# The scan's two gate projections as seven block products per pair of chunks

## The chip, the cores and the metric

The kernel runs on one core of one Trainium2 chip, as one launch. The metric is device microseconds of that launch, the median of several runs. Five engines of the core work beside each other: PE (TensorE, matmuls; PEld is its weight load), DVE (VectorE), ACT (ScalarE), POOL (GpSimd) and SP (SyncE, which here only issues DMAs). Data lives in DRAM, in SBUF (128 partitions) and in PSUM, where matmuls write; the kernel divides it in eight banks of 128 x 512 float32.

## The reference, cut to what matters

One layer over 4096 positions of width 1024. The input is normed and projected; half of the columns (group A) go through a matrix memory with four heads of 128, scanned in chunks of 128 positions in both directions; the other half (group B) through windowed attention. What the change touches are the columns `o_a` and `z_a` of the projection, 512 each:

```python
hn = rms_norm(x, norm_w)                      # [1, 4096, 1024]
proj = hn @ w_in                              # columns 1536:2048 are o_a, 2048:2560 z_a, 2560:3072 z_b (after a reorder of w_in's columns)
h = sigmoid(o_a) * (h_fwd + h_bwd)            # h_fwd, h_bwd: mLSTM over chunks of 128
h = h * rsqrt(mean(h * h) + EPS) * mhn_w      # per head
y_a = h * silu(z_a)
y_b = windowed_gqa(q_b, k_b, v_b) * silu(z_b)
x + concat([y_a, y_b]) @ w_out                # and a last rms_norm
```

So for a pair of chunks the gates are a product of a 2 x 2 block matrix with another: rows are the two chunks, the inner blocks the halves of the 1024 inputs, and columns o and z.

## The kernel before, in words

The kernel's matmuls of 128x512 take fp32r operands, and to keep float32's accuracy each operand is split into a high part (a cast by ACT) and a low part (what the cast left, by DVE or POOL), and each product is three matmuls: one with the low input, one with the low weight, one with both high parts. A full product of 128 positions with 512 columns is 8 blocks of K times 3, 24 matmuls of 128x512 that add up in one PSUM bank.

The program has four stages. Pass 1 (to about 590 us) norms the input in groups of 256 positions, splits it (`splits`, tiles `xT`), stores both parts in DRAM (`xT_d`), and does the projections of group B and its attention. Pass 2 (about 590 to 1167) goes backward over eight blocks of 512 positions: v, q and k of group A, the short convolution, and the state of the backward scan. Pass 3, the scan, is 32 chunks forward. The tail (from about 1700) does the gates of group B (`zunits`) and the output projection, which already works with seven block products per pair (`OutPair`).

In the scan a chunk n has these steps. `scores` multiplies lq and lk into a bank (S), and DVE multiplies S into the decays E in both directions. `heads` makes, per head, num = W x state + E x v for both directions (4 matmuls of 128x129); DVE takes the denominators (r), ACT scales the forward half into hs, DVE adds the backward one, multiplies the gate o in and, after the norm (ss3, with a power on POOL), the gate z. `yout` transposes hs on PE (yp), ACT copies it (ya), POOL stores it. `state` carries the running state CC on, `weigh_q` makes W = W x lq for two chunks ahead, and `proj` makes the gates: 24 matmuls op and 24 zp per chunk (L1262), a tanh on ACT and, for z, one DVE operation (L1272).

PE's order is the order in which the code issues (a manual schedule); `interleave` deals the steps of a chunk (`pieces`) evenly between its matmuls (`fill`). The other engines' orders are set by a list scheduler. All loads of the scan go through SP's queue in program order, and a load whose buffer isn't free holds up all behind it. Buffers are pools of tiles by tag: `x4` (`xtile`, 4 KB per partition) and `w8` (`wtile`, 8 KB) are shared by all passes; lq, lk, lv and lkf have two buffers each.

The inputs of the gates (`xs`, both parts) come from DRAM per pair of chunks, those of the first pair are still in SBUF; the weights (`w3`) are split by ACT and DVE at the end of pass 2 (`next_weights`). The weights of z_b, which the tail needs, are split a little at a time over the chunks (`zweight`, `zsplit`).

```python
c.psum({"pj": 2, "n": 2, "c": 1, "y": 1})      # PSUM: gates, num (2 banks each), S, yp
```

## Time and profile before

| what | value |
|---|---|
| median of 3 runs | 2185.28 us (2182.06 to 2185.89) |
| the profiled execution, its span | 2182.1 us |
| PE busy | 2156.9 us (99%), 12226 matmuls |
| DVE / ACT / POOL busy | 1416.9 (65%) / 1079.3 (49%) / 567.7 (26%) |
| op and zp in the scan (L1262), busy | 202.3 and 187.9 us, 720 records each |
| xs loads (SP) | 120 of 256 KB, 6.6 us from issue to landing |

The profiled execution took as long as its span, the least of the three times. Matmuls overlap, so the busy time of one (0.39 to 0.41 us for 128x512) is longer than the distance to the next; some records are missing (720 of 768). The chain that ended last is the one to read first, then the busy times by stage. A number in the column of idle time tells what an engine waited for, and costs nothing where the engine has time.

### The profile page before, as it was taken

The numbers are of one execution on the slowest core, as the hardware profiler recorded it, in microseconds if no ns is written. First come the engines' busy times: TensorE is split into PE (matmuls) and PEld (weight loads), VectorE is DVE, ScalarE is ACT, GpSimd is POOL, SyncE is SP. The second block draws the span as 40 slices with busy tenths as digits, with TensorE's granted clock in tenths as the row PEclk, the third lists the DMA queues.
The fourth block names the chain that finished last, engine by engine and source line by source line (L and its number), as shares of the span: only waits on it lengthen the run. The fifth ranks groups of instructions, "written<-read, shape, count | busy, mean of one in ns | idle before, by whom it ended". The sixth has DMA issues, their size and how long they took to land. (4 is left out here: it accounts for less than half of the span.)

```text
span 2182.1 us, 34919 instructions
## 1 busy us (share of the span) xinstructions
PE 2156.9 (99%) x12226; PEld 1872.4 (86%) x12226; DVE 1416.9 (65%) x3041; ACT 1079.3 (49%) x2650; POOL 567.7 (26%) x918
## 2 busy tenths in 40 slices
...
GB/s 277 158 171 147 128 173 122 130 124 64 102 148 78 141 163 135 62 160 160 113 163 230 290 259 238 211 253 225 214 238 188 329 359 283 181 177 191 193 191 147
DMA packets 249132, 398.96 MB, mean 183 GB/s; under 512 B 21979, under 2 KB 128475, under 8 KB 248956
## 3 DMA queue, kind: packets, MB, share of 16 engines
...
## 5 line engine op out<-in xcount | busy, mean ns | idle before, releaser
L932 PE MATMUL up<-xb,w 128*128 128x512 f32 x1344 | 338.4, 396 | 0.0
L1443 PE MATMUL o<-wo,yo 128*128 128x512 f32 (+1 forms) x1356 | 312.8, 393 | 0.0
L1443 PEld LDWEIGHTS o<-wo,yo 128*128 128x128 f32 x1356 | 253.2, 188 | 59.7
L932 PEld LDWEIGHTS up<-xb,w 128*128 128x128 f32 x1344 | 243.8, 188 | 47.2
L950 DVE SCALAR_TENSOR_TENSOR qk<-U,cw,qk 128x512 f32<-128x512 f32 x256 | 189.2, 752 | 91.1 <-ACT qk L948 85.8
L548 PE MATMUL qp<-xT,wqb 128*128 128x256 f32 x1536 | 242.4, 288 | 0.1
L548 PEld LDWEIGHTS qp<-xT,wqb 128*128 128x128 f32 x1536 | 214.2, 190 | 8.7 <-DVE wqb L319 0.5
L1262 PE MATMUL op<-w,xs 128*128 128x512 f32 x720 | 202.3, 408 | 0.0
L1262 PE MATMUL zp<-w,xs 128*128 128x512 f32 x720 | 187.9, 401 | 0.7 <-DVE z L1272 0.7
L905 PE MATMUL v2p<-w,xb 128*128 128x512 f32 x672 | 157.6, 395 | 0.0
L1262 PEld LDWEIGHTS zp<-w,xs 128*128 128x128 f32 x720 | 130.9, 189 | 27.4 <-DVE z L1272 1.1
L414 DVE TENSOR_TENSOR pt<-tp,pt 128x512 fp32r<-128x512 f32 x188 | 129.1, 687 | 37.7 <-ACT pt L413 35.2
L905 PEld LDWEIGHTS v2p<-w,xb 128*128 128x128 f32 x672 | 126.1, 188 | 30.1 <-DMA xb<-xT_d 0.5
L391 ACT ACTIVATE s<-s,NG 128x320 f32<-128x320 f32 (+1 forms) x256 | 139.8, 548 | 11.4 <-DVE NG L389 10.8
L1262 PEld LDWEIGHTS op<-w,xs 128*128 128x128 f32 x720 | 126.7, 189 | 21.4
L413 ACT CAST pt<-tp 128x512 fp32r<-128x512 f32 x188 | 110.5, 588 | 69.9 <-PE tp L411 67.6
L382 DVE CUSTOM_DVE_ANT_0 s<-sp,G 128x320 f32<-128x320 f32 (+1 forms) x256 | 122.2, 478 | 32.6 <-PE sp L379 29.9
L1229 ACT ACTIVATE hs<-num,r 128x128 f32<-128x128 f32 x128 | 47.0, 368 | 174.3 <-DVE r L1226 153.6
L425 PE MATMUL op<-pt,v 128*128 128x512 f32 x376 | 120.6, 402 | 5.9 <-DVE ab L438 5.8
L379 PE MATMUL sp<-kk,q 128*128 128x320 f32 (+2 forms) x512 | 118.8, 313 | 0.7 <-DVE kk L501 0.6
L411 PE MATMUL tp<-ident,s 128*128 128x128 f32 x752 | 113.2, 273 | 0.3 <-DVE pt L414 0.2
L1252 POOL DMA_DIRECT2D y_d<-ya x32 | 19.4, 607 | 329.8 <-ACT ya L1251 181.8
(275 smaller groups left out, 4480.5 us busy)
## 6 DMA issues: line engine op xcount, KB each, us to landing
...
xs<-xT_d SPq DMA_DIRECT2D x120, 256.0 KB, 6.6
xT_d<-xT POOLq DMA_DIRECT2D x104, 256.0 KB, 5.0
...
E<-m_d SPq DMA_DIRECT2D x64, 256.0 KB, 4.9
W<-w_d SPq DMA_DIRECT2D x64, 256.0 KB, 5.9
...
```

Of the source, the lines that this page charges most:

```text
L379: nc.tensor.matmul(sp[:, lo:hi], qt, kk[:, kv, z, col - 128 + lo:col - 128 + hi], start=(z == 0), stop=(z == 1))
L382: nc.vector.tensor_tensor_reduce(out=s[:, lo:hi], in0=sp[:, lo:hi], in1=bias[0][:, kv * 2 + m, lo - 64 * half:hi - 64 * half], op0=ALU.add ...
L391: LAST["act"] = nc.scalar.activation(ps[g][:, kept(g)], ps[g][:, kept(g)], AF.Exp, bias=ng[:, g:g + 1], accum_out=rs[:, g:g + 1])
L411: nc.tensor.transpose(tp[:, g * 128:(g + 1) * 128], ps[g][:, j * 128:(j + 1) * 128], c.ident)
L414: nc.vector.tensor_sub(pt[:, 1, :], tp, f32(pt[:, 0, :]))
L425: nc.tensor.matmul(op, vt, pt[:, z, :], start=(i == 0 and z == 0), stop=(i == len(js) - 1 and z == 1))
L548: nc.tensor.matmul(qp, wq[k // 2][:, k % 2, w, m * 128:m * 128 + 128], x[k], start=(k == 0 and j == 0), stop=(k == KT - 1 and j == 2))
L905: nc.tensor.matmul(vp, a, wv[k // 2][:, k % 2, m, :], start=(k == 0 and j == 0), stop=(k == KT - 1 and j == 2))
L932: nc.tensor.matmul(up[:, 0:hi - lo], w[k // 2][:, k % 2, a, cs], x, start=(k == 0 and j == 0), stop=(k == KT - 1 and j == 2))
L950: nc.vector.scalar_tensor_tensor(acc, U[:, t:t + 512], cw[:, cm, t:t + 1], acc, ALU.mult, ALU.add)
L1262: nc.tensor.matmul(P[nm], XS[n](a, k), w[:, m, :], start=(k == 0 and j == 0), stop=(k == KT - 1 and j == 2))
L1443: nc.tensor.matmul(p, a[:, z, k, :], w[k // 2][:, k % 2, m, lo:hi], start=k == 0 and z == 1, stop=k == 3 and z == 0 and m == 0)
```

## The change

The gates of two chunks are seven block products of half the depth (4 blocks of K times 3 = 12 matmuls each) instead of four of 24. With inputs x00, x01 (the halves of K of the first chunk), x10, x11 and weights in the same way, the seven inputs are four blocks and sums of them, and the seven weights too; the sums of results are built up in SBUF as the products come out.

- **Matmuls**: `pair` makes P0 to P6 (L1422), 84 matmuls per pair instead of 96. Each P is evicted when its 12th matmul is done: P0 by an ACT copy, the others by DVE additions (seven in all); the z gates then get a tanh by ACT into `th` and a product by DVE from SBUF, the o gates a tanh in place.
- **Input sums**: in pass 1 POOL makes four sums per group (`block_sums`) from the unsplit tiles and stores those and the first block in DRAM (`xo_d`); the first three groups, which are past by then, get theirs in pass 2 (`xunit`; the first pair's are split there and stored in `x0_d`). In the scan `raw` loads them unsplit, and `split` makes both parts of an operand shortly before it is used: the cast by ACT, the low part by DVE for P0, P2, P4, P6 and by POOL for P1, P3, P5. `xT_d` is stored in another layout, one store for both parts.
- **Weight sums**: 16 units in pass 2 (`wunit`) scale, add and split the weights and store them in DRAM (`wt_d`); `opweights` loads them as 14 tiles of 1 MB at the end of pass 2 and the start of the scan. The 16 splits of `next_weights` go away.
- **Start of the scan**: E, W and CC of chunk 0, operands and weights are loaded between the last products of pass 2 (`seam`).
- **Banks and buffers**: `pj` has three banks; `yp` has none of its own and shares that of S. lk and lkf have one buffer instead of two, E comes from the shared pool, the gates have six buffers. The loads of a chunk are issued in another order.
- **z_b's weights** are split in chunk 29 (`zweights`) instead of over the chunks; the first 12 units of `zunits` move to chunk 30.

The core of the diff:

```diff
@@ pass1 @@
+                for h, x in enumerate(RAW[b]):
+                    nc.gpsimd.dma_start(c.xo_d[b, h], x)
...
+            def sums():
+                LAST["pool"] = block_sums(c, RAW[b])
+                for h, x in enumerate(RAW[b]):
+                    nc.gpsimd.dma_start(c.xo_d[b, 2 + h], x)
+                    load_raw(b + 1, h)
...
-            for z in range(2):
-                q = nc.sync if b < 3 else nc.gpsimd
-                q.dma_start(c.xT_d[z, 2 * kk:2 * kk + 2, :, t0:t0 + 256].rearrange("k p t -> p k t"),
-                            f32(xt[:, :, z, 2:]))
+            q = nc.sync if b < 3 else nc.gpsimd
+            q.dma_start(c.xT_d[kk, :, :, t0:t0 + 256], f32(xt[:, :, :, 2:]).rearrange("p k z t -> p (k z) t"))
...
+def block_sums(c, r):
+    nc = c.nc
+    (a, d), (b, e) = [(x[:, :, 0:128], x[:, :, 128:256]) for x in r]
+    nc.gpsimd.tensor_tensor(out=a, in0=a, in1=d, op=ALU.subtract)
+    nc.gpsimd.tensor_tensor(out=d, in0=d, in1=e, op=ALU.add)
+    nc.gpsimd.tensor_tensor(out=e, in0=e, in1=a, op=ALU.subtract)
+    return nc.gpsimd.tensor_tensor(out=b, in0=b, in1=e, op=ALU.subtract)
@@ pass2 @@
+        SIDE = [xunit(2), xunit(1), xunit(0)] + [wunit(z) for z in range(16)]
...
+        def seam(k):
...
+            return ([op(1)], [op(2), w(4, 0)], [op(3)], [ld("e"), w(4, 1)], [ld("w")], [ld("cc"), w(5, 0)], [op(4)],
+                    [w(5, 1)])[k]
...
-                at.append((37 / 96, lambda: c.next_weights(1, (0, 1))))
-                at += [((39 + 8 * i) / 96, lambda i=i: w1(2 + i)) for i in range(2)]
+                at += [((4 + 8 * z) / 96, lambda z=z: opweights(c, 2 + z // 2, z % 2)) for z in range(4)]
@@ pass3 @@
-        c.psum({"pj": 2, "n": 2, "c": 1, "y": 1})
+        c.psum({"pj": 3, "n": 2, "c": 1})
...
+        BUFS = {"k": 1, "q": 2, "kf": 1, "v": 2}
...
-            yp = c.ps("y", [128, NH, 128], f"yp{n}")
+            yp = c.ps("c", [128, NH, 128], f"yp{n}")
...
+            nc.scalar.copy(op[:, :, 0, :], x)
+            (nc.gpsimd if i % 2 else nc.vector).tensor_tensor(out=op[:, :, 1, :], in0=x, in1=f32(op[:, :, 0, :]),
+                                                              op=ALU.subtract)
...
+                    if i == 0:
+                        nc.scalar.copy(new("o", n), p)
+                    elif i == 1:
+                        add(new("o", n + 1), p, get("o", n))
+                    elif i == 2:
+                        add(new("z", n), p, get("o", n + 1))
+                    elif i == 3:
+                        add(new("z", n + 1), p, get("z", n))
+                        add(get("o", n + 1), p, get("o", n + 1))
+                    elif i == 4:
+                        add(get("z", n), p, get("z", n))
+                    else:
+                        o = get("o", n + i - 5)
+                        add(o, p, o)
+                        TZ["t"] = nc.scalar.activation(o, o, AF.Tanh, scale=0.5)
+                if i in (3, 4):
+                    silu(n + 4 - i)
...
-        load(0, ("x", "k", "q"))
+        for j in range(2):
+            opweights(c, 6, j, wk)
...
+        load(0, ("k", "v", "kf", "q"))
...
+        for u in take(60):
             u()
...
-            load(n + 2, ("w", "v", "kf"))
-            load(n + 3, ("x", "e", "cc"))
+            load(n + 2, ("cc", "e", "w", "q"))
             if n + 2 < NCH:
                 state(m)
-            fill = (proj(m) if n else p1[24:]) if m < NCH else []
+            load(n + 2, ("kf",))
+            fill = take(42)
...
             if m < NCH:
-                pieces.append(lambda: scores(m))
+                pieces.append(lambda: (scores(m), load(n + 2, ("k",))))
```

Three places show how instructions stand now. The first is PE in a middle chunk of the scan, around the transposes yp and the scores S (names: P6_0 is product 0 of pair 6, wt its weights, op its operand; the waits name what the instruction is released by). Before:

```order
L1262 MATMUL zp12_15242<-w3_10_12954,xs12_0_14812 128x512 [waits DVE_49]
L1262 MATMUL zp12_15242<-w3_10_12954,xs12_0_14812 128x512 x5
L1249 MATMUL yp10_15250<-ident_83,hs10_15025 128x128 [waits PE_49]
L1249 MATMUL yp10_15250<-ident_83,hs10_15025 128x128
L1249 MATMUL yp10_15250<-ident_83,hs10_15025 128x128 [waits DVE_49] x2
L1262 MATMUL zp12_15242<-w3_11_12961,xs12_1_14815 128x512 x6
L1262 MATMUL zp12_15242<-w3_12_12984,xs12_2_14818 128x512 x3
L1190 MATMUL S12_15271<-lq12_14944,lk12_14946 128x128 [waits DMAHW5_49,DMAHW4_49,PE_49]
```

and now:

```order
L1422 MATMUL P6_0_15469<-wt0_0_12998,op6_0_15424 128x512 [waits DVE_49]
L1422 MATMUL P6_0_15469<-wt0_0_12998,op6_0_15424 128x512 [waits Activation_49]
L1422 MATMUL P6_0_15469<-wt0_0_12998,op6_0_15424 128x512 x3
L1349 MATMUL yp9_15481<-ident_86,hs9_15240 128x128 [waits DVE_49,PE_49]
L1349 MATMUL yp9_15481<-ident_86,hs9_15240 128x128 [waits DVE_49] x3
L1422 MATMUL P6_0_15469<-wt0_0_12998,op6_0_15424 128x512
L1422 MATMUL P6_0_15469<-wt0_0_12998,op6_0_15424 128x512 x3
L1290 MATMUL S11_15493<-lq11_15189,lk11_15333 128x128 [waits DMAHW3_49,DMAHW1_49,Activation_49]
```

S stands four matmuls behind yp now instead of nine, and waits for ACT, which copies yp out of the bank. The second place is DVE at the same point, from the decays of chunk 12 or 11 on (hs, ss3 and r as told above, W13 and lq13 are two chunks ahead). Before:

```order
L1192 TENSOR_TENSOR E12_14824<-S12_15271,E12_14824 128x512 [waits DMAHW7_49,PE_49]
L1192 TENSOR_TENSOR E12_14824<-S12_15271,E12_14824 128x512 [waits DMAHW0_49]
L1239 TENSOR_SCALAR ss3_11_15225<-ss3_11_15225 128x4 [waits Activation_49]
L1204 TENSOR_TENSOR W14_15290<-W14_15290,lq14_15262 128x1024 [waits DMAHW6_49,DMAHW4_49,DMAHW3_49]
L1242 SCALAR_TENSOR_TENSOR hs11_15190<-hs11_15190,ss3_11_15225,z11_15122 128x128 [waits Pool_49]
```

and now:

```order
L1292 TENSOR_TENSOR E11_15183<-S11_15493,E11_15183 128x512 [waits PE_49]
L1292 TENSOR_TENSOR E11_15183<-S11_15493,E11_15183 128x512
L1330 SCALAR_TENSOR_TENSOR hs10_15410<-num10_2_15429,r10_1_15443,hs10_15410 128x128 [waits Activation_49] x2
L1403 TENSOR_TENSOR o13_15553<-P6_1_15507,o12_15505 128x512 [waits PE_49]
L1334 SCALAR_TENSOR_TENSOR hs10_15410<-o10_15169,hs10_15410 128x512 [waits DVE_49]
L1304 TENSOR_TENSOR W13_15522<-W13_15522,lq13_15525 128x1024 [waits DMAHW7_49,DMAHW4_49,DMAHW3_49]
L1377 TENSOR_TENSOR op6_4_15628<-r6_3_15389,op6_4_15628 128x4x128 [waits DMAHW5_49,Activation_49]
L1339 TENSOR_SCALAR ss3_10_15452<-ss3_10_15452 128x4 [waits Activation_49]
```

The low part of an operand (L1377) and the sums out of PSUM (L1403) stand between the steps of the heads, and the wait for lq's load stands ahead of them. The third is SP's queue at the end of pass 2, from the last three stores of q on. Before:

```order
L955 DMA q_d_74<-qk0_1_13023 128x4x128 [waits DMAHW3_49,DVE_49]
L955 DMA q_d_74<-qk0_2_13119 128x4x128 [waits DMAHW4_49,DVE_49]
L955 DMA q_d_74<-qk0_3_13199 128x4x128 [waits DMAHW5_49,DVE_49]
L1155 DMA lk0_13221<-k_d_75 128x512 [waits DMAHW6_49,PE_49]
L1155 DMA lq0_13223<-q_d_74 128x512 [waits DMAHW5_49,DMAHW4_49,DMAHW7_49,DMAHW3_49,PE_49]
```

and now:

```order
L1038 DMA q_d_74<-qk0_2_13499 128x4x128 [waits DMAHW2_49,DVE_49]
L1038 DMA q_d_74<-qk0_3_13515 128x4x128 [waits DMAHW3_49,DVE_49]
L1172 DMA wt6_0_13535<-wt_d_85 128x2048 [waits DMAHW4_49]
L1172 DMA wt6_1_13537<-wt_d_85 128x2048 [waits DMAHW5_49]
L1265 DMA lk0_13542<-k_d_75 128x512 [waits DMASW4_49,DMAHW6_49,Activation_49,Pool_49]
L1265 DMA lv0_13544<-v_d_77 128x516 [waits DMAHW7_49]
L1265 DMA lkf0_13546<-kf_d_76 128x516 [waits DMAHW2_49,DMAHW3_49,DMAHW0_49,DMASW1_49]
L1265 DMA lq0_13548<-q_d_74 128x512 [waits DMAHW1_49]
```

Two weight tiles of 1 MB stand ahead of the loads of chunk 0 now, and lq0 comes last of the four.

364 lines of the change are left out of this document (233 added, 131 removed).

## The prediction

> **What bounds the kernel now.** I read the page's head first, then the table of stages, then PE at the seam between projections and scan.
>
> ```profile
> span 2182.1 us, 34919 instructions
> PE 2156.9 (99%) x12226; PEld 1872.4 (86%) x12226; DVE 1416.9 (65%) x3041; ACT 1079.3 (49%) x2650; POOL 567.7 (26%) x918
> PE 45%; DMA 1%; DVE 1%; SPq 0%; issue 0%; ACT 0%; POOLq 0%; POOL 0%; ACTq 0%; DVEq 0%
> ```
>
> The reader is to see that TensorE is idle for 25 us of 2182, and that the chain that ended last is matmuls and little else. By stages (columns: stretch, length, busy us of PE, PEld, DVE, ACT and POOL with counts, granted clock, DMA share, GB/s):
>
> ```profile
> 60.00:590.00 530.00, 523.13 (x3870) 499.17 (x3869) 420.54 (x1091) 412.50 (x1085) 246.06 (x358) 1.00 0.43 128
> 640.00:1150.00 510.00, 510.00 (x2418) 421.28 (x2417) 312.57 (x478) 204.05 (x367) 96.78 (x217) 1.00 0.42 135
> 1200.00:1648.00 448.00, 448.00 (x2571) 387.44 (x2571) 242.33 (x686) 204.13 (x667) 84.24 (x117) 1.00 0.77 241
> 1180.00:1220.00 40.00, 39.66 (x230) 34.16 (x229) 24.75 (x67) 16.96 (x56) 7.66 (x11) 1.00 1.05 361
> ```
>
> The third row is the scan: PE busy without a gap, DVE 54%, ACT 46%, POOL 19%, DMA 0.77. The fourth is its beginning, where the DMA engines are full at 361 GB/s. So matmuls taken out of the scan come off the span one for one, until something that is covered now comes out from under them.
>
> **The matmuls.** A product over all of K now takes 24 matmuls of 128x512, a block product 12. A pair of chunks has four of the first (96) or seven of the second (84); 16 pairs make 1536 against 1344, and the instruction lists of both programs have exactly these. The price is the spacing on PE, since one matmul's 0.4 us overlaps the next:
>
> ```profile
> 1167.25 5.75 PE L1262 MATMUL op<-w,xb 128*128 128x512 f32 x24
> 1172.83 5.75 PE L1262 MATMUL zp<-w,xb 128*128 128x512 f32 x24
> 1178.42 5.75 PE L1262 MATMUL op<-w,xb 128*128 128x512 f32 x24
> 1184.00 1.05 PE L1190 MATMUL S<-lq,lk 128*128 128x128 f32 x8
> ```
>
> From 1167.25 to 1184.00 stand 72 matmuls: 0.2327 us each. 192 x 0.2327 = **44.7 us off**. All else on PE (num, S, yp) stays in number.
>
> **What the engines of the scan get in exchange.** Per pair DVE gains seven additions out of PSUM, four low halves of operands and two gate products, and loses two; ACT gains seven casts; POOL three low halves:
>
> ```profile
> L1457 DVE TENSOR_TENSOR xr<-o,xr 128x512 f32<-128x512 f32 x64 | 43.3, 682 | 2.0 <-PE o L1443 1.9
> L1432 DVE TENSOR_TENSOR yo<-s,yo 128x512 fp32r<-128x512 f32 x64 | 42.7, 687 | 49.5 <-ACT yo L1431 49.4
> L1272 DVE SCALAR_TENSOR_TENSOR z<-z,zp 128x512 f32<-128x512 f32 x32 | 21.7, 680 | 1.7 <-ACT z L1270 1.7
> L1431 ACT CAST yo<-s 128x512 fp32r<-128x512 f32 x64 | 37.6, 612 | 10.4 <-DVE s L1421 9.9 <-PE o L1443 0.5
> L276 POOL TENSOR_TENSOR xT<-xraw,xT 128x512 fp32r<-128x512 f32 x52 | 57.0, 1097 | 98.7 <-ACT xT L275 83.0 <-ACT pt L413 7.6 <-PE sp L379 7.6
> L1249 PE MATMUL yp<-ident,hs x128: 270/272/329, 1206.3 to 1701.1; 128*128 128x128 f32 x128
> ```
>
> The last row gives a chunk's period: (1701.1 - 1206.3) / 31 = 15.96 us, a pair 31.9; the pair after has 31.9 - 2.8 = 29.1. DVE: 0.541 x 31.9 = 17.3, plus 7 x 0.68 + 4 x 0.69 + 2 x 0.68 - 2 x 0.68 = 7.5, so 24.8 of 29.1 (85%). ACT 14.5 + 7 x 0.61 = 18.8 (65%). POOL 6.0 + 3.3 (32%). DMA hardly changes: 2.0 MB of inputs per pair become 1.8. No engine passes PE by its sum alone, but DVE and ACT hand to each other all through a chunk, and what was 46% idle is now 15%.
>
> **The wait that is new in the scan.** yp and S now share one bank, so S waits for ACT's copy of yp, which stands behind a scale of the heads, which stands on DVE behind W, which waits for lq; and lq's load stands on SP behind lk's, which has one buffer and waits for the last S. The prices:
>
> ```profile
> 1346.17 0.38 PE L1214 MATMUL num<-CC,W 128*128 128x129 f32 x2
> 1346.98 1.18 PE L1262 MATMUL op<-w,xs 128*128 128x512 f32 x4
> 1350.99 0.60 PE L1249 MATMUL yp<-ident,hs 128*128 128x128 f32 x4
> 1351.35 2.33 PE L1262 MATMUL zp<-w,xs 128*128 128x512 f32 x9
> 1353.52 1.05 PE L1190 MATMUL S<-lq,lk 128*128 128x128 f32 x8
> 1351.63 0.59 ACT L1251 COPY ya<-yp 128x512 f32<-128x512 f32 x1 [0.74 <-PE yp L1249]
> 1355.98 0.33 SPq L1155 DMA_DIRECT2D lq<-q_d  x1
> 1363.70 1.23 DVE L1204 TENSOR_TENSOR W<-W,lq 128x1024 f32<-128x1024 f32 x1 [4.32 <-DMA lq<-q_d]
> 1366.95 1.13 DVE L1197 SCALAR_TENSOR_TENSOR CC<-CC,decay,lkf 128x129 f32<-128x129 f32 x4
> 1347.80 0.35 DVE L1230 SCALAR_TENSOR_TENSOR hs<-num,r,hs 128x128 f32<-128x128 f32 x1 [0.50 <-ACT hs L1229]
> DVE W L1204 <- DMA lq<-q_d: 83.7, 23, 5.3
> lq<-q_d SPq DMA_DIRECT2D x32, 256.0 KB, 6.1
> ```
>
> From S in P_0 to S in P_4 PE has 42 matmuls at the scan's spacing (1351.35 to 1353.52 for nine, 0.241), four num groups of 0.81 and a yp of 0.36: 13.7 us. Against it stand 0.9 for the two issues, L for lq's landing, then W 1.2, a low half 0.7, r 0.5, hs 0.8, four hs 1.2, the P_2 sum 0.6, hs 0.3, CC 1.1, r 0.5, ACT's hs 0.4 and ya 0.6: 8.8 + L. PE waits when L is over 4.9. The way from S in P_4 to the next pair's S has the same length and 7.6 of work, so it bears 6.1. L was 6.1 in the median, behind transfers of xs; now 1 MB of E and W stands ahead of it and the inputs behind. I take 5.5: 0.6 us per pair, **9.6 us**. Its ends are 0 (L under 4.9) and, with the 7.7 us between the rows 1355.98 and 1363.70, (2.8 + 1.6) x 16 = 70. It cannot be a gain, as PE has no wait there to lose.
>
> **The seam.** The operands of the first chunks lay in SBUF; now they, and 14 MB of split weights, come by DMA.
>
> ```profile
> 1173.94 2.40 DMA q_d<-qk
> ```
>
> SP holds wt6 and all behind it until the last q_d stores go out: 6.7 us after the seam at 1167.25, perhaps 6 without the weight splits that kept DVE busy. From there stand in the queue wt6 (2.1 MB), lk, lv, lkf, lq (1.05), E1, W1, CC1 (1.3), an input block and op5 (0.8): 5.25 MB, at 361 GB/s 14.5 us, so op5 lands at about 20.5. PE wants lq0 at 14, has it at 16; wants op5 at 17, has it at 20.5 to 21; op6, 2.4 MB further, lands at 27 where PE wants it at 24.6. 2 + 4 + 2 = **8 us on**; ends 0 (all in time) and 20 (those 7.6 MB all in the open). [...]
>
> **The rest.** The 16 weight splits at the seam and the eight in the scan go away; PE had no wait there, so this saves nothing. The split of wz moves into chunk 29: eight at 0.75 on a DVE with 2 us left per chunk, 2.6 us over, of which I count **2** (0 to 4). In pass 1 POOL does 13 x 4 halves of 1.1 us more, its eight stores per group stay eight; cover is its own idle time before the splits:
>
> ```profile
> L105 DVE SCALAR_TENSOR_TENSOR w<-w3s,nw,w x8: 743/746/753, 1215.9 to 1332.1; 128x512 fp32r<-128x512 f32 x8
> 307.48 1.09 POOL L276 TENSOR_TENSOR xT<-xraw,xT 128x512 fp32r<-128x512 f32 x1 [7.49 <-ACT xT L275]
> 341.12 1.09 POOL L276 TENSOR_TENSOR xT<-xraw,xT 128x512 fp32r<-128x512 f32 x1 [7.59 <-ACT pt L413]
> ```
>
> A group takes 33.6 us, 4.4 more fit into the 7.5. What is late if they don't is the input tile: raw tiles keep their two of 14 buffers longer, and ACT's pt copies need three. **2 us** (0 to 12: one pt copy late by 0.9 per group). In pass 2 the weight sums bring some 40 us to DVE, 30 to ACT, 25 to POOL, spread by hand over a stage in which DVE idles 197 us and PE not at all: 0 (0 to 5).
>
> Sum: -44.7 + 9.6 + 8 + 2 + 2 = -23.1 on the profiled span of 2182.1, which is the lowest of the three times (2182.06) with nothing around it; the median is 3.2 above. **2185.3 - 23.1 = 2162.**
>
> **Rivals.**
> (a) All of it stays hidden, 2141 to 2150, say 2144: for it speaks that the last stage runs seven products per pair with DVE adding and no wait on PE; against it the full DMA at the seam. 0.20.
> (b) DVE is blocked by POOL and becomes the bound. Two rows of pass 2 side by side:
>
> ```profile
> 706.16 1.16 POOL L1004 TENSOR_TENSOR wvr<-v,TM 128x516 f32<-128x516 f32 x1 [0.36 <-PE up L932]
> 706.33 1.55 DVE L1004 TENSOR_TENSOR wvr<-v,TM 128x516 f32<-128x516 f32 x1
> L1004 DVE TENSOR_TENSOR wvr<-v,TM x28: 680/696/1549, 656.2 to 1156.5; 128x516 f32<-128x516 f32 x28
> ```
>
> The same DVE instruction takes 0.70 alone and 1.55 when it starts inside POOL's. Three low halves of 1.1 on POOL per pair can add 3.3 to DVE's 24.8: 28.1 of 29.1, with ACT's answers (0.5 before each hs) over it; I put the pair at 30.6, 1.5 x 16 = 24 in place of 9.6: 2176. [...] 0.18.
> (c) Slower: lq lands late in every chunk. It decides where (L - 4.9) + (L - 6.1) passes (44.7 - 12) / 16 = 2.0, at L = 6.5. At 7: 3.0 x 16 = 48, 2201. For it speaks the 6.1 of before, against it that raw inputs now stand behind lq. 0.15.
> (d) Gains and losses cancel, within 0.2% (4.4 us, about what a measurement of this kernel can tell from no change): 0.07, part of it the top of (b).
>
> My forecast, 2150 to 2172 by its own terms, has 0.38; 0.02 are left for other ways to be faster. Faster 0.78, same 0.07, slower 0.15. Range: 2142 (all hidden) to 2190 (the edge of slower), outside it 0.15 above and 0.03 below.
>
> **What would show it.** Matmuls P 1344 with 0.23 to 0.24 spacing; yp about 14.6 to 14.9 us apart (over 15.3: b or c); PE idle at P_0_5 and P_0_6 released by DMA of op, some 8 us within 30 us of the seam; S waiting for ACT's ya; W waiting for lq; DVE near 24 to 25 us per pair, with stretched instructions under (b); PE in the two earlier passes as before. It would be wrong if SP is held longer than its rows say by buffers that free late, which no view of before shows.

## The result and the profile after

The changed kernel takes 2250.5 us (median of four runs, 2248.7 to 2253.1) against 2185.5: ratio 1.030 [1.029, 1.032], slower by 3%. The forecast was 2162, faster. The profiled execution has a span of 2250.5; that of before was the fastest of its kernel, so the two profiles lie 68.4 us apart where the medians lie 65.0.

The head of the page, and of its chain:

```profile
span 2250.5 us, 35346 instructions
PE 2144.5 (95%) x12034; PEld 1851.3 (82%) x12034; DVE 1574.2 (70%) x3279; ACT 1151.8 (51%) x2805; POOL 749.4 (33%) x1083
PE 33%; DMA 4%; DVE 4%; issue 1%; ACT 1%; POOL 0%; SPq 0%; POOLq 0%; ACTq 0%; DVEq 0%
```

The 192 matmuls are gone (12226 to 12034; no record of the gates is missing: the 48 of op and the 48 of zp that the table of before lacks are the first pair's, which read xb and stand under another name), but PE is idle for 106 us now where it was for 25. The table of stages, cut like that of before (pass 1, pass 2, scan, the start of the scan):

```profile
60.00:605.00 545.00, 524.81 (x3850) 497.47 (x3849) 426.82 (x1085) 411.41 (x1084) 303.19 (x404) 1.00 0.50 175
650.00:1215.00 565.00, 535.73 (x2515) 440.56 (x2514) 360.34 (x568) 227.39 (x422) 168.81 (x296) 0.98 0.61 191
1290.00:1745.00 455.00, 431.98 (x2471) 369.23 (x2470) 349.00 (x852) 259.17 (x784) 138.16 (x155) 0.99 0.72 231
1225.00:1285.00 60.00, 45.90 (x215) 37.85 (x214) 32.96 (x67) 21.27 (x56) 11.81 (x16) 0.86 0.93 321
```

The second row is the surprise: pass 2, where PE had no gap, has 29 us of gaps in this stretch, at a granted clock of 0.98. For the account I cut each trace at four events of PE: the first product of pass 2 (up), the first product of the scan (op before, P now), the first and the last yp.

| us | pass 1 | pass 2 | seam | scan | tail | span |
|---|---|---|---|---|---|---|
| before | 587.8 | 579.4 | 39.1 | 494.8 | 481.0 | 2182.1 |
| after | 605.7 | 619.5 | 59.6 | 485.9 | 479.8 | 2250.5 |
| difference | +17.9 | +40.1 | +20.5 | -8.9 | -1.2 | +68.4 |
| forecast | +2 | 0 | +8 | -33 in scan and tail | | -23 |

So 58.0 of the 68.4 us were lost before the first matmul of the part that the change is about, and the scan itself gave 8.9 where 33 were forecast.

**Pass 2.** PE's three gaps of the worst stretch, DVE's row before the first and POOL's rows before that; then one of PE's later gaps with ACT's rows at it, and ACT's line in the table of waits (columns: start, length, instruction, and in brackets the idle time before it with its releaser; in the table the sum, the number and the longest). ktp is the transpose of k, kv a product for the state, wvh and wvl are the two parts of the weighted v, v2p is the projection of v, u the input of an input-sum unit, wu the weights of a weight unit:

```profile
725.87 1.12 PE L1082 MATMUL ktp<-ident,qk 128*128 128x128 f32 x4 [9.88 <-DVE kt L1085]
732.14 0.39 PE L151 MATMUL kv<-wvh,kt 128*128 128x258 f32 x1 [2.59 <-ACT wvh L1097]
735.03 0.58 PE L152 MATMUL kv<-wvl,kt 128*128 128x258 f32 x1 [2.50 <-DVE wvl L1098]
711.10 7.14 DVE L1033 SCALAR_TENSOR_TENSOR qk<-U,cw,qk 128x512 f32<-128x512 f32 x4 [7.24 <-POOL U L1027]
701.59 1.73 POOL L681 TENSOR_TENSOR u<-u 128x512 f32<-128x512 f32 x1 [3.51 <-DMA u<-xT_d]
710.88 0.19 POOL L1027 COPY U<-hl 128x4 f32<-128x4 f32 x1
931.98 12.05 PE L988 MATMUL v2p<-w,xb 128*128 128x512 f32 x45 [2.80 <-ACT v L994]
930.95 0.51 ACT L955 ACTIVATE wu<-wu,nw 128x256 f32<-128x256 f32 x1 [1.10 <-DMA wu<-w_in]
931.37 0.56 ACT L994 COPY v<-v2p 128x512 f32<-128x512 f32 x1
ACT wu L955 <- DMA wu<-w_in: 47.3, 15, 6.5
```

DVE waits 7.2 us for POOL's copy of the convolution's edge (U, L1027), and POOL gets to it only behind input sums, for two of which it waits itself until accumulating loads of u have landed (3.51, and 1.87 at 705.78). Further on, ACT waits for a weight tile (wu) that has just been asked for, in all 47.3 us in 15 waits; its copy of v stands behind that, and PE behind the copy, four times for 9.6 us in all.

**Pass 1.** The reading of one group's end, DVE and PE:

```profile
214.05 1.80 DVE L386 SCALAR_TENSOR_TENSOR NG<-st,nsink 128x4 f32<-128x4 f32 x1
221.31 0.16 DVE L386 SCALAR_TENSOR_TENSOR NG<-st,nsink 128x4 f32<-128x4 f32 x1
237.84 0.63 PE L408 MATMUL tp<-ident,s 128*128 128x128 f32 x4 [1.00 <-DVE pt L411]
```

NG, four numbers per partition, takes 0.16 us or 1.80. ACT's exponentials wait for it (39.5 us in 28 waits over the pass), and behind them PE's transposes.

**The seam.** PE from the first product on:

```profile
1225.22 8.52 PE L1422 MATMUL P<-wt,op 128*128 128x512 f32 x36
1238.42 7.41 PE L1422 MATMUL P<-wt,op 128*128 128x512 f32 x24 [4.68 <-ACT o L1401]
1251.62 2.08 PE L1290 MATMUL S<-lq,lk 128*128 128x128 f32 x8 [5.80 <-DMA lq<-q_d]
1256.99 4.18 PE L1422 MATMUL P<-wt,op 128*128 128x512 f32 x9 [3.29 <-DVE CC L1297]
1263.85 0.73 PE L1422 MATMUL P<-wt,op 128*128 128x512 f32 x2 [0.33 <-DMA op<-xT_d]
```

and the clock that was granted there:

```profile
1225.23:1238.42 13.19, 8.51 (x38) 6.58 (x36) 8.22 (x13) 6.25 (x15) 3.18 (x6) 1.00 1.03 388
1251.00:1256.50 5.50, 2.08 (x8) 1.78 (x8) 4.51 (x8) 2.83 (x9) 2.03 (x2) 0.50 1.09 321
1256.50:1263.00 6.50, 6.01 (x19) 5.14 (x20) 1.92 (x2) 0.24 (x1) 1.22 (x2) 0.53 1.08 340
```

Three waits make 13.8 us, and behind each of them the granted clock is 0.50 for a while (from 1238.80 to 1242.10, and from 1249.00 to 1262.60 around the other two): nine P from 1256.99 to 1260.97 are 0.44 apart. Two rows of the chain that ended last (start, length) show what the second wait hangs on:

```profile
1236.32 6.70 DMA q_d<-qk
1243.46 8.12 DMA lq<-q_d
```

The last store of q is sent 11.1 us after the seam's first product and needs 6.70 to land; by that chain lq's load goes out behind it, and it lands at 1251.58, 26.4 us after the first product. The seam holds about as many products as before (131 against 126), so its 20.5 stand against the forecast's 8.

**The scan.** yp is 15.67 us apart, not 14.6 to 14.9:

```profile
L1349 PE MATMUL yp<-ident,hs x128: 270/273/422, 1284.8 to 1770.7; 128*128 128x128 f32 x128
1413.48 1.16 PE L1290 MATMUL S<-lq,lk 128*128 128x128 f32 x8 [0.72 <-ACT ya L1351]
1412.85 0.58 ACT L1351 COPY ya<-yp 128x512 f32<-128x512 f32 x1
1412.58 0.37 ACT L1329 ACTIVATE hs<-num,r 128x128 f32<-128x128 f32 x1 [2.88 <-DVE r L1326]
1405.57 1.23 DVE L1304 TENSOR_TENSOR W<-W,lq 128x1024 f32<-128x1024 f32 x1 [0.19 <-DMA lq<-q_d]
1696.09 1.23 PE L1290 MATMUL S<-lq,lk 128*128 128x128 f32 x4 [2.33 <-ACT ya L1351]
1688.19 1.23 DVE L1304 TENSOR_TENSOR W<-W,lq 128x1024 f32<-128x1024 f32 x1 [2.75 <-DMA lq<-q_d]
PE S L1290 <- ACT ya L1351: 18.4, 13, 2.3
PE P L1422 <- DVE op L1377: 4.6, 1, 4.6
```

S does wait for ya as forecast: 18.4 us in 13 waits between 1290 and 1740, 20.7 in 14 over the whole scan, in every second chunk. The first four rows below yp's are one such chunk, from S back to W, and the next two are another's S and W. ya stands behind hs, hs behind r, and r behind what DVE does from W on. This chain is rigid: in all 14 chunks S starts 7.9 to 8.0 us after W. W itself had just waited, in 11 of the 14 by the profile for lq's landing. In these chunks W started 6.2 to 8.0 us after lq's load was issued (6.9 in the mean), in the others 4.0 to 6.4, and there S did not wait for ya. The 4.6 for an operand is a single wait, and it stands in chunk 29, among the splits of z_b's weights (eight on DVE from 1722.3 to 1735.1). ACT's casts of the operand (from 1727.75) follow a wait for the load of those weights:

```profile
1730.83 1.65 PE L1422 MATMUL P<-wt,op 128*128 128x512 f32 x3 [4.64 <-DVE op L1377]
1726.27 1.33 ACT L107 ACTIVATE w<-w3s,nw 128x512 fp32r<-128x512 f32 x2 [3.38 <-DMA w3s<-w_in]
```

The granted clock drops here too: behind the wait of 2.15 for ya that ends at 1631.02 it is 0.50 from 1631.35 to 1634.60.

### The profile page after: what moved, and what is told of

The parts are those of the page before. It is cut to its first block, busy times and chain, and to the rows that moved or that the text cites. A ratio compares the mean times of both kernels' runs of the same rounds, so it can differ in the third digit from the quotient of the medians.

```text
span 2250.5 us, 35346 instructions
## 1 busy us (share of the span) xinstructions
PE 2144.5 (95%) x12034; PEld 1851.3 (82%) x12034; DVE 1574.2 (70%) x3279; ACT 1151.8 (51%) x2805; POOL 749.4 (33%) x1083
## 5 line engine op out<-in xcount | busy, mean ns | idle before, releaser
L1422 PE MATMUL P<-wt,op 128*128 128x512 f32 x1344 | 366.3, 413 | 12.9 <-ACT o L1401 4.7
L1422 PEld LDWEIGHTS P<-wt,op 128*128 128x128 f32 x1344 | 245.1, 194 | 59.0 <-ACT o L1401 5.1
L1033 DVE SCALAR_TENSOR_TENSOR qk<-U,cw,qk 128x512 f32<-128x512 f32 x256 | 199.8, 795 | 77.9 <-ACT qk L1031 50.3
L988 PE MATMUL v2p<-w,xb 128*128 128x512 f32 x672 | 163.7, 404 | 11.2 <-ACT v L994 9.6
L388 ACT ACTIVATE s<-s,NG 128x320 f32<-128x320 f32 (+1 forms) x256 | 140.2, 550 | 40.3 <-DVE NG L386 39.5
L408 PE MATMUL tp<-ident,s 128*128 128x128 f32 x752 | 114.0, 274 | 12.4 <-DVE pt L411 12.4
L151 PE MATMUL zbp<-xc,w 128*128 128x512 f32 x256 | 101.8, 398 | 0.7 <-DVE az L1229 0.7
L1376 ACT CAST op<-r 128x512 fp32r<-128x512 f32 x105 | 64.8, 618 | 72.5 <-PE P L1422 34.1
L153 PE MATMUL zbp<-xc,w 128*128 128x512 f32 x256 | 101.1, 395 | 0.0
L152 PE MATMUL zbp<-xc,w 128*128 128x512 f32 x256 | 101.0, 395 | 0.0
```

Of the source, the lines that this page charges most:

```text
L151: nc.tensor.matmul(out, wl, xh, start=first, stop=False)
L152: nc.tensor.matmul(out, wh, xl, start=False, stop=False)
L153: nc.tensor.matmul(out, wh, xh, start=False, stop=last)
L388: LAST["act"] = nc.scalar.activation(ps[g][:, kept(g)], ps[g][:, kept(g)], AF.Exp, bias=ng[:, g:g + 1], accum_out=rs[:, g:g + 1])
L988: nc.tensor.matmul(vp, a, wv[k // 2][:, k % 2, m, :], start=(k == 0 and j == 0), stop=(k == KT - 1 and j == 2))
L1033: nc.vector.scalar_tensor_tensor(acc, U[:, t:t + 512], cw[:, cm, t:t + 1], acc, ALU.mult, ALU.add)
```

## The experiments

The stages follow one another, so one run can change several and each is read by its own stretch. How far that goes the stages show that a run left alone: five runs with the changed kernel's own pass 2 gave 616 to 622, its seam 59 to 61, its scan 485 to 493. Less than 5 us in pass 2, 2 in the seam or 9 in the scan is therefore no finding by one run. Only D1 was timed in several runs. All stages in us:

| run | pass 1 | pass 2 | seam | scan | tail |
|---|---|---|---|---|---|
| A1 sums off | 605.1 | 596.2 | 60.1 | 488.1 | 480.6 |
| A2 sums on DVE | 623.0 | 603.0 | 60.2 | 487.3 | 480.5 |
| A3 other work on POOL | 633.9 | 610.3 | 61.0 | 475.3 | 480.7 |
| A4 loads ahead | 606.0 | 625.1 | 65.7 | 488.7 | 479.5 |
| B1 NG, late yp | 612.7 | 609.0 | 58.2 | 491.0 | 479.2 |
| B2 old places | 649.2 | 604.7 | 61.4 | 478.1 | 481.2 |
| B3 both | 607.7 | 604.9 | 59.0 | 496.1 | 482.4 |
| C1 all off | 595.6 | 586.3 | 52.5 | 475.4 | 480.4 |
| C2 late sums | 632.2 | 625.2 | 60.5 | 480.1 | 482.7 |
| C3 low halves on POOL | 617.7 | 587.6 | 59.2 | 543.2 | 479.7 |
| D1 best of all | 612.3 | 588.6 | 57.8 | 474.0 | 479.7 |
| D2 light scan | 595.1 | 582.2 | 49.4 | 471.9 | 482.6 |
| E1 no stores, no sums | 602.0 | 621.5 | 60.0 | 493.2 | 482.6 |
| E2 sums, no stores | 604.4 | 621.5 | 59.2 | 484.9 | 479.7 |
| E3 old places, no stores | 587.5 | 618.1 | 60.6 | 486.2 | 480.0 |
| E4 stores by SP | 594.9 | 616.4 | 59.9 | 484.7 | 481.1 |

(B1, B2, B3, D1 and D2 put the first yp 17 P and 8 S, 4.8 us of matmuls, later in PE's order and leave the last where it was; the table has moved that much from their seam to their scan.)

### Pass 2: what the units cost

A1 takes the work out of the input-sum units (accumulating loads and sums; their other loads and the stores stay) and the sums out of pass 1; it also gives ACT's copy ya priority. A2 takes the arithmetic out of the weight units (their stores stay; their loads bring twice the bytes in longer runs, and ACT no longer waits for them), makes pass 1's sums on DVE, and gives yp a bank of its own at the cost of one of P's three:

```diff
 A1
-                LAST["pool"] = block_sums(c, RAW[b])
...
-                        nc.gpsimd.dma_start(r[i][:, 2 * z:2 * z + 2], c.xT_d[...], accum_op=ALU.add)
...
-                block_sums(c, r)
...
+            with tc.high_priority(offset=EV):
+                nc.scalar.copy(ya, yp)
 A2
-                LAST["pool"] = block_sums(c, RAW[b])
+                block_sums(c, RAW[b], nc.vector)
...
             def sums():                 # of a weight unit
+                store(T["u"][:, 0:7], 0)
...
-        c.psum({"pj": 3, "n": 2, "c": 1})
+        c.psum({"pj": 2, "n": 2, "c": 1, "y": 1})
```

> Changed kernel with three edits, one in each of three stages, read stage by stage: the four input sums per group in pass 1 are left out (their stores stay); the three input-sum units of pass 2 keep loads and stores but add nothing and do no sums; ACT's copy of yp gets priority in the scan. Theory: in pass 1 it is POOL's added arithmetic that blocks DVE, so the first matmul of pass 2 comes at 588 to 591 us (605.7 in the changed kernel, 587.8 before); if the added transfers are the cause it stays at 603 to 606. In pass 2 the three units hold POOL's queue, so the stage (619.5 us, 579.4 before) falls to 590 to 597; if the weight units are the cause it stays above 612. In the scan S waits for the late copy of yp, so the time from the first to the last yp (485.9 us) falls to 460 to 468; if DVE is the bound it stays at 482 to 487.

> Changed kernel with three edits: pass 1's input sums run on DVE instead of POOL; the weight units of pass 2 only load and store (no scaling, sums or splits); yp has its own bank again and the products two instead of three. Theory: DVE has 0.7 us per sum and no longer waits for POOL, so pass 2 begins at 588 to 596 us; if transfers are the cause, 603 to 606; if DVE has no room, above 606. Pass 2: the weight units cost what is left beside the input sums, some 12 to 18 us, so 601 to 608 of 619.5; if they cost nothing, 617 to 620. Scan, first to last yp: 465 to 475 of 485.9, the wait for the copy gone, but a product waits for the eviction of the one before the last; DVE as the bound: 482 or more.

Pass 2 fell by 23.3 without the work of the input sums (596.2) and by 16.5 without that of the weight units (603.0); the two add up to 39.8 of the 40.1. With both taken out in one run it fell by 33.2 (C1) and 37.2 (D2), so up to 7 may be the loads and stores that stay. PE's waits, first of A1, then of A2, for the stretch 606 to 1225:

```profile
PE v2p L983 <- ACT v L989: 9.9, 4, 3.2
```

```profile
PE ktp L1070 <- DVE kt L1073: 12.1, 4, 9.3
```

Each run keeps just the gap of the units that it left alone: A1 the waits for v behind the weight tiles, A2 the 9.3 us of kt behind the edge copies. What the losses hold beyond the waits stands at a lower clock; the changed kernel around its gap of 9.88, and as long a stretch of the kernel before around the same matmuls (clock in the third column from the end):

```profile
690.00:766.00 76.00, 61.04 (x276) 49.97 (x275) 51.14 (x66) 26.30 (x48) 38.46 (x57) 0.89 0.75 228
```

```profile
655.00:731.00 76.00, 76.00 (x361) 62.77 (x360) 46.54 (x71) 30.70 (x56) 13.55 (x33) 1.00 0.43 136
```

Pass 1 and scan of both are taken up below.

What makes the units dear: A3 keeps them but loads both parts and adds on DVE in place of the accumulating DMA; A4 loads a weight unit ahead of its use and keeps the accumulating DMA without the sums. Of the scan's start and steps A3 changes the distance from yp to S (a step more) and the banks of the first two products, A4 the order of SP's loads (wt6 last) and ya's priority.

```diff
 A3
-                        nc.gpsimd.dma_start(r[i][:, 2 * z:2 * z + 2], c.xT_d[...], accum_op=ALU.add)
+                    nc.vector.tensor_add(r[i], r[i], lo[i])
...
+    for x in r:                        # pass 1, in place of the sums: as long, with one input
+        for y in (x[:, :, 0:128], x[:, :, 128:256]):
+            for _ in range(2):
+                ins = c.nc.gpsimd.affine_select(out=y, in_=y, ...)
...
+                pieces.append(lambda: None)
                 pieces.append(lambda: (scores(m), load(n + 2, ("k",))))
-                pieces.append(lambda: None)
...
+                    P[i] = c.ps("n", ...)[:, 0] if j == 0 and i < 2 else c.ps("pj", ...)
 A4
+        for z in range(16):
+            SIDE += [W[z + 1][0]] if z < 15 else []
...
-        load(0, ("k", "v", "kf", "q"))
+        load(0, ("q", "k"))
+        c.ops0[5] = operand0(c, 5)
+        load(0, ("v", "kf"))
```

> Changed kernel with four edits: pass 1's four sums on POOL are replaced by eight instructions of one input each (masks over the same tiles), about as long together; the three input-sum units of pass 2 load both parts and add and sum on DVE; in the scan one more share of matmuls stands between yp and S; the first two products of the scan use the idle banks of num. Theory: if DVE is held up only where POOL's instruction has two inputs, pass 2 begins at 588 to 592 us; if any POOL instruction holds it, or POOL's queue is simply late, at 602 to 607. Pass 2: POOL's queue is free of waits for loads, 590 to 600 of 619.5. Scan, first to last yp: 462 to 470 of 485.9; 482 to 487 if DVE bounds. From the first product to the first yp: 59.6 falls to 48 to 54, the wait of 4.7 and the low clock behind it gone.

> Changed kernel with four edits: the weight units of pass 2 load one unit ahead; its input-sum units do no sums but still add the low parts by transfers that POOL issues; ACT's copy of yp has priority; at the start of the scan lq, lk and the sixth operand are loaded first and the last weights behind W1 and CC1. Pass 1 is as in the changed kernel: pass 2 begins at 605 to 607 us. Theory for pass 2: the transfers that wait for loads hold POOL's queue more than the sums do, so the stretch from 690 to 760 us still loses over 10 us; if the sums are the cause it loses under 5. ACT no longer waits for weight loads, so the rest of the stage loses under 8 us. Scan, first to last yp: 460 to 468 of 485.9. From the first product to the first yp: 59.6 falls to 48 to 53, the waits of S for lq and of the sixth product for its operand gone (9 us), the wait for the eviction of the first one kept.

A3's pass 2 is 9.2 shorter, A4's no shorter (625.1): without the sums, PE still waits 8.8 us for ktp in two gaps, so the accumulating loads and what hangs on them are a part of that cost. A load one unit ahead on SP isn't earlier where SP's queue itself is held: in the changed kernel's trace four stores of k hold it for 33 us, waiting for DVE:

```profile
698.02 33.47 SPq L1038 DMA_DIRECT2D k_d<-qk  x4
SPq L1038 <- DVE qk L1036: 39.8, 4, 18.2
```

So B1 and B3 send the weight tiles by ACT's queue, B2 by POOL's (with the input sums on DVE as in A3, and their loads by ACT's queue); B2 and B3 leave empty steps behind the units' loads; C2 leaves them on SP but among the products of q and k only; C3 sends them by ACT's queue and puts the input-sum units at the end of pass 1:

```diff
 B1, B3, C3, D1
-                    nc.sync.dma_start(u[:, sl, :], src[:, :, g * 128:g * 128 + 128])
+                    nc.scalar.dma_start(u[:, sl, :], src[:, :, g * 128:g * 128 + 128])
 C3, D1
-        SIDE = [xunit(2), xunit(1), xunit(0)] + [wunit(z) for z in range(16)]
+        SIDE = [wunit(z) for z in range(16)]
...
+        hooks += [(5 + 6 * i, f) for i, f in enumerate(f for j in (2, 1, 0) for f in xunit(c, j))]
```

B1 took 609.0, so ACT's queue alone is worth 10; B2 604.7 and B3 604.9; C2 gained nothing (625.2). C3 took 587.6 (and D1, with the same, 588.6), with 5 more in pass 1 (617.7 against B1's 612.7). The same units with the same arithmetic cost 40 us where they were and in C3 some 13 in the other place and queue. In D1, where pass 1's stores go by SP, they may cost up to 22: the last part of its pass 1, in which the units stand, is 13.1 longer than in D2, which has neither them nor sums. In C3's form the price is set by what stands behind the units in each engine's order, and their work is the smaller part.

### Pass 1: places, stores and a held instruction

A1 says that the sums are not it: without them 605.1. A2 (sums on DVE, 623.0) and A3 (as much work with one input on POOL, 633.9) are worse. A1's trace shows what DVE waits for, NG and POOL's rows beside it:

```profile
214.09 2.94 DVE L385 SCALAR_TENSOR_TENSOR NG<-st,nsink 128x4 f32<-128x4 f32 x1
214.02 1.15 POOL L271 TENSOR_TENSOR xT<-xraw,xT 128x512 fp32r<-128x512 f32 x1
215.06 0.81 POOL L286 DMA_DIRECT2D xT_d<-xT  x1
215.75 1.25 POOL L271 TENSOR_TENSOR xT<-xraw,xT 128x512 fp32r<-128x512 f32 x1
```

NG starts inside one split of POOL's, outlasts a DMA issue, and ends with the next split (214.09 + 2.94 = 217.03). B1 and B3 make NG as four instructions with one tensor each, B2 and B3 put the splits back at their old places with the sums behind them, C2 makes the sums in the next group:

```diff
 B1, B3, C3
-            nc.vector.scalar_tensor_tensor(ng, mx, -1.0, nsink..., ALU.mult, ALU.min)
+            for z in range(4):
+                nc.vector.tensor_scalar(ng[:, z:z + 1], mx[:, z:z + 1], -1.0, nsink...[:, z:z + 1], ALU.mult, ALU.min)
 B2, B3
-(8, 15, 22, 29, 33)
+(12, 20, 28, 36, 40)
 C2
-(8, 15, 22, 29, 33)
+(12, 20, 28, 36)
...
+        A1 += s1[:5] + [lambda: scale_raw(b + 3)] + s1[5:] + [lambda: late_sums(b + 2)]
```

> Changed kernel with five edits, read by stage. Pass 1: the row minimum NG, a DVE instruction of two tensor inputs that took up to 2.9 us beside POOL's splits, is four instructions of one tensor and a scalar column each; all else there stays. If POOL's instructions block DVE only when DVE has two tensor inputs, pass 2 begins at 588 to 595 us (605.7 in the changed kernel); if the block is not the cause, 604 to 608. Pass 2: the loads of the weight units go by ACT's queue, not behind SP's stores, so 7 to 15 of 619.5 us come back, 604 to 612; if their arithmetic is the cause, 617 to 621. Scan: yp moves behind the scores, so S waits for no copy; first to last yp 462 to 468 of 485.9; if DVE's chain is the bound, 478 to 487. From the first product to the first yp (which now comes some 5 us later in the order, 64 us): operands 5 and 6 are loaded ahead of q's last stores and the first two products have banks of their own; 50 to 57 if the late loads are the cause, 62 or more if DRAM bandwidth bounds it.

> Changed kernel with five edits. Pass 1: the four splits are back at the places they had before the change (matmul 12, 20, 28 and 36 of a group's 40 instead of 8, 15, 22 and 29) and the sums behind them. If it was the splits' new place that put them on DVE's row minimum, pass 2 begins at 590 to 597 us of 605.7; if the sums or transfers are the cause, 602 to 608. Pass 2: the three input-sum units load both parts by ACT's queue with three empty steps behind, and add on DVE; the weight units load by POOL's queue: 590 to 602 of 619.5 if waits for loads on in-order queues are the cause, above 612 if not. Scan: yp behind the scores as in the other kernel, and all low halves on DVE: 460 to 468 of 485.9 if POOL's share blocks DVE, 468 to 476 if DVE's added 2 us per pair cost more than the block.

> Changed kernel with both edits of pass 1 (splits back in place, row minimum with one tensor input): 587 to 591 us of 605.7 if the block of DVE is the whole cause; 595 or more if something else holds part of it. Pass 2: input-sum units as in the changed kernel but with three empty steps behind the load and behind the accumulation, weight loads by ACT's queue: 594 to 604 of 619.5 if the time to the load is what matters; 610 or more if POOL's own work does. Scan: yp behind the scores, and lq's load ahead of those of CC, E and W: 458 to 465 of 485.9; no change against the kernel without that (462 to 468) if DVE's wait for lq does not matter. Start of the scan as in the first kernel but with three banks: 4 to 6 us more than it.

> Everything is computed. Pass 1: splits and loads at their old places, the sums of a group in the q phase of the next, where POOL is idle for 7 us. If it is POOL's place beside DVE's two-input instructions that counts, pass 2 begins at 590 to 598 us of 605.7; if raw tiles held longer make the loads late, above 606. Pass 2: the weight units run only among the q and k products, where no copy of v stands behind ACT's wait for a load: 606 to 612 of 619.5; 617 or more if the wait only moves. Scan: the only edit is that all low halves are on DVE; 470 to 478 of 485.9 if POOL's low halves block DVE, 484 to 492 if not.

None is better than the changed kernel's 605.7 (612.7, 649.2, 607.7, 632.2). In pass 1 B2 and B3 differ by the form of NG alone, and B3 is 41.5 shorter: none of its NG rows of one tensor took over 0.22 us (0.19 to 0.22), where those of B2 took 0.83 in the mean. At the splits' new places the same edit did not pay (B1, 7.0 longer): four rows of 0.21 cost more than one held row, 0.62 in the mean, and v, which DVE also makes from two tensors, rose from 0.73 to 1.17. NG's hold is thus real, but it is not the whole cost. With the sums behind splits at the old places PE waits three times as long for pt, another DVE product; B2, and the changed kernel:

```profile
PE tp L408 <- DVE pt L411: 38.6, 15, 4.0
```

```profile
PE tp L408 <- DVE pt L411: 12.4, 15, 1.2
```

C1 takes everything out at once, and two pairs with the unsplit blocks' stores out (the scan then loads plain input blocks) separate the rest:

```diff
 E1 (E2: the sums stay; E3: splits at 12, 20, 28, 36; E4: see the last lines)
-                    nc.gpsimd.dma_start(c.xo_d[b, h], x)
...
-                LAST["pool"] = block_sums(c, RAW[b])
-                    nc.gpsimd.dma_start(c.xo_d[b, 2 + h], x)
...
-                nc.sync.dma_start(x, c.xo_d[j, t])
+                nc.sync.dma_start(x, A["xt"][j, :, 4 * (t % 2):4 * (t % 2) + 4, :])
 E4, also
-            q = nc.sync if b < 3 else nc.gpsimd
-            q.dma_start(c.xT_d[kk, :, :, t0:t0 + 256], ...)
+            nc.sync.dma_start(c.xT_d[kk, :, :, t0:t0 + 256], ...)
```

> Pass 1 without the stores of the unsplit blocks and without the sums (the scan loads the plain input blocks in their place, as many bytes); splits and input loads stay at the changed kernel's places, the units of pass 2 stay. To the first product of pass 2 it was 587.8 us before, 605.7 changed, 605.1 with the stores but without the sums, 595.1 with the stores on SP's queue and without the sums. Theory T, that the stores cost it (a raw tile's shared buffer isn't free until its store has landed, and ACT's pt waits for that; POOL spends its time on issuing them): 587 to 592. Rival R, that the new places of the splits cost it by themselves, by POOL against DVE: 602 to 606. Pass 2 as in the changed kernel, 616 to 624.

> As the run beside it, but POOL makes the four sums per group and only the stores are left out. Theory T (stores are the cost, the sums at their new places cost 0.6 as measured with stores): 588 to 594. Rival R2, that sums or stores, each alone, are enough to make POOL the one that holds up DVE at the group's end: 600 to 606.

> Pass 1 with the splits at their old places, no sums, no stores of the unsplit blocks (the scan loads plain input blocks in their place). It differs from the kernel before in pass 1 only in the layout of the split input's stores and the moment of the input's loads. Theory N (the new places put POOL's splits and its DMA issues back to back, and DVE's NG and v, with two SBUF inputs, wait for all of them; the old places do not): NG's mean near 0.31 to 0.33 us as before, pass 1 588 to 591; if the stores of the unsplit tiles are what the old places still cost, it falls from 595.6 to that; rival, that the store's layout or the loads cost it: 594 to 597.

> Pass 1 with the splits at the changed kernel's places, no sums, no stores of the unsplit blocks, and the stores of the split input issued by SP in place of POOL. Only the issuing queue differs from the run without sums and stores that took 602.0. Theory N: without POOL's DMA issues between its splits DVE gets in between them: NG's mean falls from 0.80 to 0.21 to 0.25 us, pass 1 588 to 593. Rival, that the splits themselves at the new places block DVE whoever issues the stores: NG stays over 0.6, pass 1 600 to 603.

E1 (602.0) refutes the theory that the stores are the cost: they are 3.1 of it at the new places. E3 (587.5) is the kernel before to 0.3 us, so neither the new layout of the split input nor the later input loads cost anything. From E3 to E1 only the places of the splits and, behind them, the loads differ: 14.5. From E1 to E4 only the queue that stores the split input differs: 7.1, and NG is nearly free again. In the groups between (from the first query product, qp, of the fourth group to that of the last) E4 took 405.1 us, as did the kernel before, and E1 419.4: with SP issuing the stores the new places cost nothing there. NG in the groups from 120 to 520, of E1 and of E4 (busy time, mean ns):

```profile
L382 DVE SCALAR_TENSOR_TENSOR NG<-st,nsink 128x4 f32<-128x4 f32 x46 | 36.8, 800 | 1.1
```

```profile
L381 DVE SCALAR_TENSOR_TENSOR NG<-st,nsink 128x4 f32<-128x4 f32 x48 | 10.1, 211 | 1.1
```

What E4 keeps over E3, 7.4, is for the most part one wait early in the pass, ACT's copy of ab behind a store on SP that now stands behind the split input's:

```profile
86.26 1.22 PE L417 MATMUL op<-pt,v 128*128 128x512 f32 x2 [6.40 <-DVE ab L430]
84.91 0.58 ACT L429 COPY ab<-op 64x512 f32<-64x512 f32 x1 [6.71 <-DMA at_d<-ab]
```

So the 18.2 over E3 are: the splits' new places, at which POOL goes from split to DMA issue to split without a pause, 14.5; the stores of the unsplit tiles 3.1 (8.1 at the old places, C1 against E3); the sums 0.6 (2.4 without stores, E2 against E1). E4 shows that it takes POOL's issues between the splits; that their delay reaches PE through DVE's held instructions is read from the rows above. Where SP issues the stores the sums cost more: D1 has 612.3 with sums and input-sum units, D2 595.1 without both; of these 17.2, 13.1 lie in the last part of the pass, where the units stand, and 4 in the groups before.

### The seam and the scan

C1 has neither sums nor the weight units' arithmetic, splits all low halves of the scan on DVE, puts a step between yp and S, and doesn't load the last three weight sets (6 MB less; the first three stand in). C2 splits all low halves on DVE; C3 splits them all on POOL, with that step between yp and S. D2 drops four of seven additions out of PSUM as well:

```diff
 C1, D2
+    if i > 3:
+        c.wt[i].append(c.wt[i - 4][j])
+        return
 C1, C2, B2, D1, D2 (C3: nc.gpsimd)
-            (nc.gpsimd if i % 2 else nc.vector).tensor_tensor(out=op[:, :, 1, :], ...)
+            nc.vector.tensor_tensor(out=op[:, :, 1, :], ...)
 B1, B2, B3, D1, D2
+            pieces = [lambda: decays(m), (lambda: yout(n - 2)) if n > 1 else (lambda: None)]
 B1, B3, D1, D2
-                    [w(5, 1)])[k]
+                    [w(5, 1), op(5), op(6)])[k]
...
-        for j in range(2):
-            opweights(c, 6, j, wk)
...
         load(0, ("k", "v", "kf", "q"))
+        for j in range(2):
+            opweights(c, 6, j, wk)
 B3
-            load(n + 2, ("cc", "e", "w", "q"))
+            load(n + 2, ("q", "cc", "e", "w"))
 D2
-                        add(get("o", n + 1), p, get("o", n + 1))
...
-                        add(get("z", n), p, get("z", n))
```

> Leaves out what was added ahead of the scan, to see whether the rest is free: in pass 1 the sums (their stores of unsummed tiles stay) and the splits' new places; in pass 2 the arithmetic of both kinds of units (their loads and stores stay); at the start of the scan the loads of the last three weight sets (the first three stand in for them). In the scan all low halves on DVE and one more share of matmuls between yp and S. If the splits' places are the cause in pass 1, pass 2 begins at 588 to 591 us; if it is the added stores and the new layout, at 602 to 606. Pass 2: the two kinds gave back 23.3 and 16.5 us of 40.0 one by one; together 579 to 582 if they add up, 585 or more if the transfers hold a part. From the first product to the first yp (59.6): 42 to 48 if 6 MB less of loads is what counts, 55 or more if the waits for evictions and for q's stores do. Scan, first to last yp: 475.3 with the gap alone; 460 to 468 if POOL's low halves block DVE, 475 to 480 if DVE's added 2 us per pair take as much.

> Everything is computed. Pass 1 with the row minimum of one tensor input (612.7 with that alone) and the three input-sum units in its last part, where POOL is nearly idle from 500 to 590 us: pass 2 begins at 612 to 620 us, and pass 2 falls by what these units cost there, from 609.1 (with ACT-queue weight loads) to 585 to 590; if the units cost the same wherever they stand, the sum of both stages stays at 1219 to 1224. Scan: all low halves on POOL and one more share of matmuls between yp and S: 475.3 with the gap alone; 480 to 500 if POOL's low halves block DVE or come late, 470 to 476 if DVE's relief of 2.8 us per pair counts.

> Leaves out: the sums of pass 1 and of pass 2's input units and the weight units' arithmetic, four of DVE's seven additions per pair in the scan, and the loads of the last three weight sets. Pass 1 has its splits at the new places and stores by SP: 605.1 with stores by POOL; 594 to 599 if POOL's issuing of stores is the cause, 603 to 607 if the traffic is. Scan: against 473.3 with the full additions; DVE gets 2.7 us per pair less. If the load of DVE is what sets the scan now, 455 to 463; if it is the order of waits and not the load, 469 to 475. Start of the scan: with 6 MB less of loads (52.5 with late operands), the operands loaded early and banks for the first products, 46 to 52 with 6 of it yp's later place; 56 or more if the waits for the last q of pass 2 bound it.

**Seam.** With 6 MB less to load it is 7.1 shorter in C1 (52.5; C2 and A3, which share C1's other edits on the scan, have 60.5 and 61.0), so the transfers are a part of it. Banks and order alone only moved the wait: A3 and A4 took 61.0 and 65.7; in A3 PE waits for op3 ahead of lq, and A4, which loads lq first, has no wait for lq and one of 14.6 for op6. With operands 5 and 6 ahead of q's last stores and wt6 behind chunk 0's loads it took 58.2, 59.0 and 57.8 (B1, B3, D1), a gain little above the scatter, and D2, with that and 6 MB less, has 49.4. Nothing came near 39.

**Scan.** ya's priority (A1, 488.1; A4, 488.7), yp's own bank (A2, 487.3, with a bank less for P) and a later yp (B1, 491.0) changed nothing that can be told from the scatter; nor did lq's load ahead of those of CC, E and W in that form, in which S waits for no copy (B3, 496.1). No run moves lq in the changed kernel's own form. A step between yp and S gave 10.6 (A3, 475.3). Low halves on DVE gave 5.8 by themselves (C2, 480.1), which is within the scatter, 17.0 beside the late yp (D1 against B1, which in the steps of the scan differ by nothing else), and nothing beside the step (C1, 475.4, against A3). All low halves on POOL, with the step, cost 68 against C1 (543.2). The waits for ya and the low halves in C3:

```profile
PE S L1295 <- ACT ya L1356: 48.2, 12, 4.9
L1382 POOL TENSOR_TENSOR op<-r,op 128x512 fp32r<-128x512 f32 x89 | 132.2, 1486 | 139.8 <-ACT op L1381 139.8
```

CC takes 0.54 us there and 0.35 in the kernel before; the low half takes POOL 1.49 and DVE 0.69. The clock is a part of the 68 too: it is 0.93 in the mean from 1270 to 1805. D2, with four additions fewer per pair, gained 2.1 over D1, less than the scatter: it isn't DVE's sum of work that holds the scan there. There PE's transposes, which share S's bank, wait for E in 12 chunks:

```profile
PE yp L1334 <- DVE E L1277: 11.3, 12, 2.6
```

### The best of all

D1 takes pass 1's stores by SP, the input-sum units at the end of pass 1, the weight units by ACT's queue, the late yp, low halves on DVE, operands 5 and 6 early and the idle banks for the first two products. It computes everything.

```diff
-                    nc.gpsimd.dma_start(c.xo_d[b, h], x)
+                    nc.sync.dma_start(c.xo_d[b, h], x)
```

> Everything is computed; the edits that helped, together. Pass 1: all stores by SP instead of POOL (eight per group, 0.55 to 0.8 us of POOL each), and the three input-sum units in its last part (5 us where it was tried). If POOL's issuing of stores is what cost the 8 us that neither places nor sums explain, pass 2 begins at 598 to 604 us; if the traffic itself, or SP's queue gets stuck on them, at 609 to 615. Pass 2 with loads of the weight units by ACT's queue and no input sums: 586 to 589 (587.6 before, in the same form). Start of the scan with operands 5 and 6 ahead of q's last stores and two more banks: 62 to 65, of which 6 is yp's later place. Scan with yp behind the scores and all low halves on DVE: 471 to 476. The whole: 2190 to 2215, some 40 to 60 less than the changed kernel and still over the 2182 of before.

2213.8 us (median of four runs), ratio to the kernel before 1.012 [1.010, 1.013]: 37 us better than the changed kernel, 26 worse than the one before. Pass 1 came out at 612.3 where 598 to 604 was expected. No version beat the kernel before by more than can be told. D2, which leaves out sums, weight units' work, four additions and 6 MB of loads, is at 2183.0 against 2188.0, so with nearly all its side work gone this change is about even.

## Why the prediction was wrong, point by point

- **44.7 us of matmuls**: right as a count (12034 matmuls, P 1344) and as work: PE's busy time fell where it wasn't waiting. It did not come off the span one for one.
- **Pass 2, 0**: measured 40.1, the largest miss. The step that failed is "spread over a stage in which DVE idles 197 us and PE not at all": idle time in sum doesn't cover a wait in an engine's order. ACT waited 47.3 us for weight tiles that SP asked for late, POOL stood on the input units ahead of the edge copies, and PE got both: 29 us of gaps in the stretch above, and the lower clock around them (0.89 in the mean from 690 to 766).
- **Pass 1, 2**: measured 17.9. I counted POOL's added halves against its idle 7.5 us; the cost was the new places of the splits, which I hadn't priced at all (14.5), by POOL's splits and DMA issues back to back against DVE: the block that rival (b) put down for the scan. In A1's rows an NG took 2.94 us, beside two splits and the DMA issue between them, where others took 0.16. That the 14.5 are this hold alone isn't shown: freeing NG of it paid at the splits' old places and not at the new ones.
- **Seam, 8**: measured 20.5. The step that failed is the time of lq: I had q's last stores sent 6 us after the seam's start and lq there at 16; the last was sent at 11.1, it needed 6.7 to land, lq's load went out behind that, and lq was there at 26.4. PE wanted it at 14, so this alone is 12.4 in place of 2. The wait of 4.7 for the eviction of P0 lies within it (three banks of twelve matmuls are full in 8.4 us, where two of 24 before lasted 11.2, and ACT's copy stood behind the decays of chunk 0): A3, with two more banks, was no shorter. op5 and op6 (4 and 2) were 3.3, in part for CC, and 0.3. Missed too was the clock: behind the waits it was 0.50 to 0.53 and the matmuls stood up to 0.44 us apart; against the same instructions before (24 of 128x512 in 5.75 us, eight S in 1.05) my estimate of that is 5.5 us. The waits and this make 19.6 of the 20.5.
- **Scan, 9.6 of new waits**: mechanism right, size wrong. S waits for ya, ya for DVE's work behind W, and W for lq, once per pair, as told: 20.7 us in 14 waits. The step that failed is "I take 5.5" for L: from lq's issue to W's start it was 6.2 to 8.0 us in the chunks that waited; their waits begin at about 5.4, not far from the 4.9 of the sum. What the sum lacked is that PE's other instructions stand further apart as well (means without waits: a P 0.250 us against 0.243 of op and zp, S 0.116 against 0.101), some 12 us over the stretch. Half of it is the clock, which stood at 0.50 for 3.4 us at each of four waits (from 1290, 1631, 1696 and 1730 on); away from these a P is at 0.246 and S at 0.110, and what holds those apart stays open. The 186 matmuls fewer between the first and the last yp are 45.1 at the old spacing; less 20.7, the 4.6 of chunk 29 and 12 this makes some 8 of gain, where 8.9 was measured.
- **Chunk 29, 2**: measured 4.6 for the operand, and a clock of 0.50 for 3.4 us behind it (1730.30 to 1733.60); the term was costed on DVE's spare time alone and left out ACT's wait for the load of those weights. This chunk lies in the scan's stretch, and every run above has this wait among the same eight splits, 3.4 to 5.7 us long; no run moved them.
- **Rival (b), DVE held up by POOL's low halves**: given 0.18, and true in its mechanism, as far as C3 shows it (CC at 0.54 us, 0.35 in the kernel before): beside the late yp, low halves off POOL gave 17.0 us, and all on POOL cost 68. As a forecast of the whole it was as wrong as mine.
- **Rival (c), slower by lq late in every chunk**: right in the sign, wrong in the cause. lq was late for S in one chunk of each pair; that is the 20.7 above, with which the scan still gained, and the kernel became slower ahead of the scan.
